# Norm sums as two matmuls with a tile of ones, rows placed later, and mLSTM preparation as a step of its own

## The chip, the cores and the metric

The kernel runs on one core of one Trainium2 chip. The metric is the device time of one execution in microseconds (us). Of the engines, PE multiplies matrices, DVE (VectorE) and ACT (ScalarE) do most elementwise work, POOL (GpSimd) a little of it, and SP only issues transfers. Each engine works off a queue of its own; the queues meet at semaphores.

## What is computed

One layer of an encoder block on 512 tokens of width 1024, in float32. Three mixers run side by side and are merged by gates.

```python
h = rms_norm(x, mix_norm_g[l])
proj = h @ w_in[l]
ml_q, ml_k, ml_v, ml_o, ml_gates, na_qkv, xa_q, merge_pre = jnp.split(proj, split_points, axis=-1)
y_ml = mlstm_branch(ml_q, ml_k, ml_v, ml_o, ml_gates, ...)
y_na = neighbourhood_attention(na_q, na_k, na_v, na_rpb[l])
mem_k, mem_v = jnp.split(rms_norm(mem, mem_norm_g[l]) @ w_mem_kv[l], 2, axis=-1)
y_xa = memory_cross_attention(xa_q, mem_k, mem_v)
merged = g_ml * (y_ml @ w_br_ml[l]) + g_na * (y_na @ w_br_na[l]) + g_xa * (y_xa @ w_br_xa[l])
x = x + merged @ w_out[l]
x = x + conv_glu_ffn(rms_norm(x, ffn_norm_g[l]), w_ffn_up[l], ...)
return rms_norm(x, final_norm_g)
```

Here `rms_norm` multiplies each token by the reciprocal root of its mean square plus 1e-6. The mLSTM branch has 4 heads of width 128 and runs in both directions; each head's 512 tokens are worked on in 4 chunks.

## The kernel before

Activations lie transposed, features on the partitions and tokens along the free axis. Every operand of a projection is split into a rounded part and the rest (`split_act` for activations: ACT copies, L209, DVE subtracts, L210; `emit_split` for weights: L185 on ACT, L186 on DVE), and each product is three matmuls (`mm3`, L203 to L205). A block of weights is loaded by SP (tile `wr`, three buffers) three blocks ahead, and split one block ahead into halves (tile `w`, four buffers). A projection `proj(key, ...)` is 8 steps over k, so 24 matmuls, of 512 columns for x and 256 for the memory tokens. The blocks come in this order: mlq (four columns of a k at a time, into four banks `mm`), mlk0 to mlk3, tm (values and gates), xaq0 to 3, o0 to o3 (output gate), memk0 to 3, memv, naq, nak, the merge gates with the branch products, out, then the FFN (ua, uu, dn).

The norm is not applied to the operand. Squares are summed over the 8 feature tiles into `acc` (tokens on the free axis), and the sum over partitions is made later: `rstd_cols` gets one column per 128 tokens (a float32 matmul with one column of ones, L285, which the profile shows as two records each), DVE scales and adds the epsilon (L287) and POOL raises to the power -0.5 (L289). `rstd_row` turns these columns into a row that stands on all partitions: two diagonal tiles (L302), two matmuls with a tile of ones (L303), a copy by ACT (L305). The row multiplies what a projection gives. That is done three times: for x inside mlk0, for the memory tokens between o1 and o3, for the FFN in its first block.

The mLSTM runs as a generator, `ml_all`. After each projection block the main program calls `step(RB)` or `step(RM)`, which adds 1.4 or 0.75 to a quota and lets the generator run to its next `yield` for each whole one. `ml_prep` makes the decays; its rows go out to DRAM (`rd`) and come back on all partitions as tiles R, loaded by SP (L564), to which POOL adds a mask (L567), giving a second tile of the same tag, four buffers in all, so one head's worth. Each head then does: `keys` (products of keys and queries, L586; keys transposed, L588, copied by ACT with a scale, L590, and by DVE, L591), `diagonal` (exponentials of the masked R by ACT, L600, times the products, L604), `states` (L626, three matmuls per direction, the first result copied by ACT, L629, the others added by DVE, L631), `queries` (exponentials of R, L613), and four times `values_J` (L642, L644) with a normalisation (L646 to L653). The next head's R is loaded right after `queries`. `emit_y` ends a head one head later: transposes (L668), a product with the gate (L670), and a split.

A scheduler orders the instructions of each engine by a model of its own; `tc.issue_after` puts instructions behind a named one.

Of the kernel before, what the change touches and what calls it, by code (L numbers as in the profile page):

```python
# [17 lines left out]
P = 128  # L18
S = 512
# [83 lines left out]
def hybrid_block(ctx, tc, xT, memT, wflat, vecs, gbias, nabias, outa, outb):  # L103
# [14 lines left out]
    def nm(s):  # L118
        uid[0] += 1
        return f"{s}_{uid[0]}"  # L120
# [13 lines left out]
    def atps():  # L134
        return atp.tile([P, 512], F32, tag="at", name=nm("at"))
# [141 lines left out]
    V.tensor_scalar(ngh, vec[:, VEC["mlng"]:VEC["mlng"] + 4], 0.5, None, op0=ALU.mult)  # L277


    def rstd_cols(acc, ntok, tag, n=D):  # L280

        nt = ntok // P
        ps = atps()
        for t in range(nt):
            PE.matmul(ps[:, t:t + 1], acc[:, t * P:(t + 1) * P], ones[:, 0:1], start=True, stop=True)  # L285
        v = tiny(nt)
        V.tensor_scalar(v, ps[:, :nt], 1.0 / n, EPS, op0=ALU.mult, op1=ALU.add)  # L287
        col = cp.tile([P, nt], F32, name=f"rc_{tag}")
        G.tensor_tensor(col, v, nhalf[:, :nt], op=ALU.pow)  # L289
        return col  # L290
# [54 lines left out]
    for k in range(KT):  # L345
# [6 lines left out]
        for f in range(4):  # L352
            fs = slice(f * P, (f + 1) * P)
            mm3(ps_q[f], wh[:, fs], wl[:, fs], XH[k], XL[k], k == 0, k == KT - 1)

    ps_k = [proj(("mlk", 0), XH, XL, bank=atps, at={1: lambda: norm.append(rstd_cols(acc, S, "x")),
                                                    7: lambda: norm.append(rstd_row(norm[0], S, "x"))})]
    rc, rb = norm
    ps_k.append(proj(("mlk", 1), XH, XL, bank=atps))
    rcc = cp.tile([P, NT], F32, name="rcc")  # L360
    V.tensor_scalar(rcc, rc, C_ML, None, op0=ALU.mult)

# [98 lines left out]
    ml = {}  # L461


    def ml_prep():
        gv = Gt.rearrange("p t (d k h) -> p t d k h", d=2, k=2)
        T4 = lambda a: a.rearrange("p (t d h) -> p t d h", t=4, d=2)
        f = tiny(32)
# [55 lines left out]
        V.tensor_tensor(rr[:36], cu[:36], mr[:36], op=ALU.subtract)  # L523
        for d in range(2):
            G.dma_start(rd[d], rr[32 * d:32 * d + 4, :])
        yield
        for d in range(2):
            for u in range(2):
                g = 2 * u + d
                gs = slice(32 * g, 32 * g + 4)  # L530
                ends = mr[gs].rearrange("p (t c) -> p t c", t=NT)[:, :, P - 1 if d == 0 else 0:][:, :, 0:1]
                V.tensor_tensor(dg[gs, g], ends.to_broadcast([4, NT, 4]),
                                ident[gs, gs].unsqueeze(1).to_broadcast([4, NT, 4]), op=ALU.mult)
# [17 lines left out]
            J, Jp = pr[d]  # L551
            V.tensor_tensor(ex[:, 1, d, J], en[:, 1, d, J], mb[:, d, Jp], op=ALU.add)
        A.activation(ex, ex, AF.Exp)
        ml.update(rd=rd, em=em, bi=bi, mb=mb, ex=ex)

    def ml_all():
        yield from ml_prep()
        rd, em, bi, mb = ml["rd"], ml["em"], ml["bi"], ml["mb"]

        def load_R(h):  # L560
            R, rm = [], []
            for d in range(2):
                t = tp.tile([P, S], F32, tag="R", name=nm("R"), bufs=4)
                SY.dma_start(t, rd[d, h].partition_broadcast(P))  # L564
                R.append(t)
                t = tp.tile([P, S], F32, tag="R", name=nm("R"), bufs=4)
                G.tensor_tensor(t.rearrange("p (j c) -> p j c", j=4), R[d].rearrange("p (j c) -> p j c", j=4),  # L567
                                msk[d].unsqueeze(1).to_broadcast([P, 4, P]), op=ALU.add)
                rm.append(t)
            return R, rm  # L570
# [93 lines left out]
        def emit_y(h, H):  # L664
# [8 lines left out]
                yml.extend([unit(F32R), unit(F32R)])  # L673
            split_act(yml[0][:, hs], yml[1][:, hs], y)

        prev = None
        R, rm = load_R(0)
        for h in range(4):
            kt, C = own(h)
            kq = keys(h, kt)  # L680
# [247 lines left out]
        mem_part(f)  # L928
        step(RB)
    for f in range(4):  # L930
        ps = proj(("o", f), XH, XL)
        t = scr()
        V.tensor_tensor(t, ps, rb, op=ALU.mult)
        A.activation(t, t, AF.Tanh, scale=0.5)
        if f == 0:
            so.append(unit())
        if f == 1:

            with tc.issue_after(st["mm"]):
                mrc = rstd_cols(macc, M, "m")  # L940
        if f == 2:
            mrb = rstd_row(mrc, M, "m")
        V.tensor_scalar(so[0][:, f * S:(f + 1) * S], t, 1.0, None, op0=ALU.add)
        step(RB)
    mkv = unit()
    mk, mv = mkv[:, 0:1024], mkv[:, 1024:2048]
    for f in range(4):
        ps = proj(("memk", f), MH, ML, M)
        V.tensor_tensor(mk[:, f * M:(f + 1) * M], ps[:, :M], mrb, op=ALU.mult)
        step(RM)  # L950
    pss = [mmps() for _ in range(2)]
    for i in range(4):
# [216 lines left out]
    for hh in range(2):  # L1169
# [3 lines left out]
        for j in range(HF):  # L1173
            f = HF * hh + j
            if f == 0:
                wa, wu = weights(("ua", f)), weights(("uu", f))
                pa, pu = mmps(), mmps()
                for k in range(KT):
                    if k < KT - 1:
                        mm3(pa, wa[k][0], wa[k][1], HH[k], HL[k], k == 0, False)  # L1180
                for k in range(KT - 1):
                    mm3(pu, wu[k][0], wu[k][1], HH[k], HL[k], k == 0, False)
                k = KT - 1
                mm3(pa, wa[k][0], wa[k][1], HH[k], HL[k], False, True)
                rc2 = rstd_cols(acc2, S, "2")
                mm3(pu, wu[k][0], wu[k][1], HH[k], HL[k], False, True)
            else:
                pa = pa1 if f == 1 else proj(("ua", f), HH, HL)
            if f == 0:
                pa1 = proj(("ua", 1), HH, HL)  # L1190
                rb2 = rstd_row(rc2, S, "2")
            c = conv(pa, rb2, "ffw", "ffb", f, FT)
            sq = scr()
            A.activation(sq, c, AF.Square)
# [131 lines left out]
```

## Time and profile before

| what | us |
|---|---|
| median of 3 runs | 887.96 |
| lowest and highest | 886.85, 888.22 |
| profiled execution | 888.33 |
| its span, first to last instruction | 886.5 |
| PE busy in the span | 875.3 |
| DVE, ACT, POOL busy | 580.3, 449.8, 165.6 |

Bytes moved to and from HBM are 98.9 MB, 112 GB/s over the span. In the profile, times in the lists of waits are the engine's idle time before a line, with what released it; a matmul's duration is that of its whole passage and longer than its distance to the next start, because matmuls overlap.

### The profile page before, as it was taken

The numbers are of one execution on the slowest core, as the hardware profiler recorded it, in microseconds if no ns is written. First come the engines' busy times: TensorE is split into PE (matmuls) and PEld (weight loads), VectorE is DVE, ScalarE is ACT, GpSimd is POOL, SyncE is SP. The second block draws the span as 40 slices with busy tenths as digits, with TensorE's granted clock in tenths as the row PEclk, the third lists the DMA queues.
The fourth block names the chain that finished last, engine by engine and source line by source line (L and its number), as shares of the span: only waits on it lengthen the run. The fifth ranks groups of instructions, "written<-read, shape, count | busy, mean of one in ns | idle before, by whom it ended". The sixth has DMA issues, their size and how long they took to land.

```text
span 886.5 us, 12192 instructions
## 1 busy us (share of the span) xinstructions
PE 875.3 (99%) x4342; PEld 741.6 (84%) x4342; DVE 580.3 (65%) x1153; ACT 449.8 (51%) x955; POOL 165.6 (19%) x238
## 2 busy tenths in 40 slices
PE   9999999999999999999999999999999999999997
PEld 7898877988888888888888888888888888888897
DVE  6794576766566747988767557667733466667433
ACT  7453446654345638888744435454422344444532
POOL 4201222110000930543000211211100011111010
PEclk9999999999999999999999999999999999999999
DMA  7324643532222534554333432232233322332412
GB/s 257 103 81 132 197 146 100 165 115 76 72 89 80 131 106 126 157 142 138 111 98 109 141 106 88 98 116 95 66 99 97 119 95 95 97 98 84 140 33 95
DMA packets 39436, 99.67 MB, mean 112 GB/s; under 512 B 5960, under 2 KB 13640, under 8 KB 39376
## 3 DMA queue, kind: packets, MB, share of 16 engines
q1 hardware_dynamic: 31728, 92.45, 32.0%
q0 software_dynamic: 7360, 6.32, 3.3%
q8 instruction: 34, 0.56, 0.3%
q14 instruction: 26, 0.21, 0.1%
q10 hardware_dynamic: 288, 0.14, 0.1%
HBM read 94.67 MB, written 4.21 MB: 112 GB/s over the span
## 4 chain that ended last, share of the span: by engine, by line
PE 94%; DMA 2%; DVE 1%; issue 1%; ACT 1%; POOL 0%; SPq 0%; POOLq 0%; DVEq 0%; ACTq 0%
PE mm L205 28%; PE mm L203 28%; PE mm L204 28%; PE at L203 2%; PE at L205 2%; PE at L204 2%; DMA R<-rd 1%; PE at L783 1%; PE at L764 1%; PE at L642 1%; PE at L644 1%; DMA s<-xT 1%; DMA rd<-s 0%; PE at L626 0%; PE at L745 0%
## 5 line engine op out<-in xcount | busy, mean ns | idle before, releaser
L203 PE MATMUL mm<-u,w 128*128 128x512 f32 (+1 forms) x1077 | 417.7, 388 | 0.4 <-ACT u L209 0.4
L205 PE MATMUL mm<-u,w 128*128 128x512 f32 (+1 forms) x1077 | 414.1, 384 | 0.1
L204 PE MATMUL mm<-u,w 128*128 128x512 f32 (+1 forms) x1077 | 413.7, 384 | 0.1
L185 ACT ACTIVATE w<-wr 128x512 fp32r<-128x512 f32 (+1 forms) x298 | 184.4, 623 | 239.7 <-PE mm L205 209.1
L186 DVE TENSOR_TENSOR w<-wr,w 128x512 fp32r<-128x512 f32 (+3 forms) x299 | 213.7, 716 | 114.4 <-ACT w L185 112.2
L205 PEld LDWEIGHTS mm<-u,w 128*128 128x128 f32 x1077 | 202.4, 188 | 40.8 <-DVE w L186 0.7
L203 PEld LDWEIGHTS mm<-u,w 128*128 128x128 f32 x1077 | 202.6, 188 | 39.6 <-ACT u L209 0.7
L204 PEld LDWEIGHTS mm<-u,w 128*128 128x128 f32 x1077 | 202.6, 188 | 39.2 <-DVE u L210 0.5
L1198 POOL TENSOR_TENSOR s<-s,rb 128x512 f32<-128x512 f32 x22 | 37.3, 1695 | 252.5 <-DVE s L1197 240.0
L457 POOL DMA_DIRECT2D u<-nav_d x128 | 62.2, 518 | 96.8 <-PE at L783 57.6
L209 ACT ACTIVATE u<-s 128x512 fp32r<-128x512 f32 x26 | 16.4, 631 | 55.3 <-DVE s L1201 54.5
L1201 DVE TENSOR_TENSOR s<-mm,s 128x512 f32<-128x512 f32 x22 | 15.2, 691 | 23.3 <-POOL s L1198 23.3
L1044 POOL TENSOR_TENSOR acc<-acc,s 128x512 f32<-128x512 f32 x7 | 9.1, 1295 | 102.7 <-ACT s L1043 102.7
L371 ACT ACTIVATE s<-pad,vec 128x512 f32<-128x512 f32 x30 | 24.4, 813 | 7.0 <-DVE pad L369 6.4
L210 DVE SCALAR_TENSOR_TENSOR u<-s,u 128x512 fp32r<-128x512 f32 x26 | 18.0, 691 | 14.7 <-ACT u L209 14.7
L372 DVE SCALAR_TENSOR_TENSOR s<-pad,vec,s 128x512 f32<-128x512 f32 x30 | 22.5, 751 | 4.3 <-ACT s L371 4.2
L1197 DVE SCALAR_TENSOR_TENSOR s<-s,s 128x512 f32<-128x512 f32 x22 | 15.2, 692 | 14.0 <-ACT s L1196 14.0
L373 DVE SCALAR_TENSOR_TENSOR s<-pad,vec,s 128x512 f32<-128x512 f32 x30 | 22.5, 751 | 0.9
L1196 ACT ACTIVATE s<-s 128x512 f32<-128x512 f32 x22 | 13.9, 632 | 16.3 <-DVE s L1195 16.2
L203 PE MATMUL mm<-w,u 128*128 128x512 f32 x48 | 19.0, 395 | 0.0
L205 PE MATMUL mm<-w,u 128*128 128x512 f32 x48 | 18.7, 390 | 0.0
L204 PE MATMUL mm<-w,u 128*128 128x512 f32 x48 | 18.7, 390 | 0.0
(285 smaller groups left out, 1028.1 us busy)
## 6 DMA issues: line engine op xcount, KB each, us to landing
wr<-wflat SPq DMA_DIRECT2D x140, 512.0 KB, 3.3
s<-xT SPq DMA_DIRECT2D x16, 256.0 KB, 4.4
nab<-nabias SPq DMA_DIRECT2D x16, 256.0 KB, 2.7
u<-nav_d POOLq DMA_DIRECT2D x128, 32.0 KB, 2.5
wr<-wflat SPq DMA_DIRECT2D x15, 192.0 KB, 2.4
nav_d<-nv POOLq DMA_DIRECT2D x8, 256.0 KB, 2.4
R<-rd SPq DMA_DIRECT2D x8, 256.0 KB, 3.8
wr<-wflat SPq DMA_DIRECT2D x2, 544.0 KB, 3.3
```

Of the source, the lines that this page charges most:

```text
L185: A.activation(h[:, u:v], src, AF.Copy)
L186: V.tensor_tensor(l[:, u:v], src, h[:, u:v].bitcast(F32), op=ALU.subtract)
L203: PE.matmul(ps, lh, rh, start=start, stop=False)
L204: PE.matmul(ps, lh, rl, start=False, stop=False)
L205: st["mm"] = PE.matmul(ps, ll, rh, start=False, stop=stop).ins
L209: A.activation(h, src, AF.Copy, scale=scale)
L210: V.scalar_tensor_tensor(l, src, scale, h.bitcast(F32), op0=ALU.mult, op1=ALU.subtract)
L371: A.activation(t1, pad[:, 0:512], AF.Identity, scale=vcol(w, i), bias=vcol(b, i))
L372: V.scalar_tensor_tensor(t1, pad[:, 1:513], vcol(w, n + i), t1, op0=ALU.mult, op1=ALU.add)
L373: V.scalar_tensor_tensor(t1, pad[:, 2:514], vcol(w, 2 * n + i), t1, op0=ALU.mult, op1=ALU.add)
L457: G.dma_start(vw[r * 32:(r + 1) * 32, i * 256:(i + 1) * 256], nav_v[hf, r, CW[b]:CW[b] + 32, hp * 256:(hp + 1) * 256])
L1198: G.tensor_tensor(c, c, rb2, op=ALU.mult)
```

## The change

`rstd_cols` is cut in two. `rstd_parts` splits the sums of squares into two rounded parts (one ACT copy, one DVE subtraction). `rstd_cols` multiplies both with a tile of ones (L291), so the sum over partitions stands on every partition for every token, and DVE takes each 128 columns times the identity and sums along the row, which picks the columns (L295); the scale and the epsilon go into the same instruction. POOL's power is L298 now.

The places change too. For x, the columns come after the fourth k of mlk0 (before: after the second), the row after the fourth k of mlk1 (before: at the end of mlk0). For the memory tokens the parts are made ahead of o2, the columns inside o2, the row in memk0, and the explicit order is gone. For the FFN the parts come before the last k of the first block, the columns after the first k of ua1, the row behind ua1 as before.

In the mLSTM, the load of head 0's R moves from after the preparation to the start of its last step, and that step now ends with a `yield`, so that head 0's keys and first diagonal come one step of the generator later, and so does everything behind them.

```diff
...
     V.tensor_scalar(ngh, vec[:, VEC["mlng"]:VEC["mlng"] + 4], 0.5, None, op0=ALU.mult)
-    def rstd_cols(acc, ntok, tag, n=D):
+    def rstd_parts(acc, ntok):
+
+        h, l = [sp.tile([P, 512], F32R, tag="scr", name=nm("s"))[:, :ntok] for _ in range(2)]
+        split_act(h, l, acc)
+        return h, l
+
+    def rstd_cols(parts, ntok, tag, n=D):
         nt = ntok // P
         ps = atps()
+        for i, part in enumerate(parts):
+            PE.matmul(ps[:, :ntok], onesr, part, start=i == 0, stop=i == 1)
+        v = tiny(nt)
+        d = scr(P)
         for t in range(nt):
-            PE.matmul(ps[:, t:t + 1], acc[:, t * P:(t + 1) * P], ones[:, 0:1], start=True, stop=True)
-        v = tiny(nt)
-        V.tensor_scalar(v, ps[:, :nt], 1.0 / n, EPS, op0=ALU.mult, op1=ALU.add)
+            V.tensor_tensor_reduce(d, ps[:, t * P:(t + 1) * P], ident, 1.0 / n, EPS, ALU.mult, ALU.add,
+                                   accum_out=v[:, t:t + 1])
         col = cp.tile([P, nt], F32, name=f"rc_{tag}")
         G.tensor_tensor(col, v, nhalf[:, :nt], op=ALU.pow)
         return col
...
             fs = slice(f * P, (f + 1) * P)
             mm3(ps_q[f], wh[:, fs], wl[:, fs], XH[k], XL[k], k == 0, k == KT - 1)
-    ps_k = [proj(("mlk", 0), XH, XL, bank=atps, at={1: lambda: norm.append(rstd_cols(acc, S, "x")),
-                                                    7: lambda: norm.append(rstd_row(norm[0], S, "x"))})]
+    xp = rstd_parts(acc, S)
+    ps_k = [proj(("mlk", 0), XH, XL, bank=atps, at={3: lambda: norm.append(rstd_cols(xp, S, "x"))}),
+            proj(("mlk", 1), XH, XL, bank=atps, at={3: lambda: norm.append(rstd_row(norm[0], S, "x"))})]
     rc, rb = norm
-    ps_k.append(proj(("mlk", 1), XH, XL, bank=atps))
     rcc = cp.tile([P, NT], F32, name="rcc")
     V.tensor_scalar(rcc, rc, C_ML, None, op0=ALU.mult)
...
     ml = {}
-    def ml_prep():
+    def ml_prep(load_R):
         gv = Gt.rearrange("p t (d k h) -> p t d k h", d=2, k=2)
         T4 = lambda a: a.rearrange("p (t d h) -> p t d h", t=4, d=2)
         f = tiny(32)
...
         V.tensor_tensor(rr[:36], cu[:36], mr[:36], op=ALU.subtract)
         for d in range(2):
             G.dma_start(rd[d], rr[32 * d:32 * d + 4, :])
+        ml["rd"] = rd
         yield
+        ml["R"] = load_R(0)
         for d in range(2):
             for u in range(2):
                 g = 2 * u + d
...
             J, Jp = pr[d]
             V.tensor_tensor(ex[:, 1, d, J], en[:, 1, d, J], mb[:, d, Jp], op=ALU.add)
         A.activation(ex, ex, AF.Exp)
-        ml.update(rd=rd, em=em, bi=bi, mb=mb, ex=ex)
+        ml.update(em=em, bi=bi, mb=mb, ex=ex)
+        yield
     def ml_all():
-        yield from ml_prep()
-        rd, em, bi, mb = ml["rd"], ml["em"], ml["bi"], ml["mb"]
         def load_R(h):
+            rd = ml["rd"]
             R, rm = [], []
             for d in range(2):
                 t = tp.tile([P, S], F32, tag="R", name=nm("R"), bufs=4)
...
                 yml.extend([unit(F32R), unit(F32R)])
             split_act(yml[0][:, hs], yml[1][:, hs], y)
+        yield from ml_prep(load_R)
+        em, bi, mb = ml["em"], ml["bi"], ml["mb"]
         prev = None
-        R, rm = load_R(0)
+        R, rm = ml["R"]
         for h in range(4):
             kt, C = own(h)
             kq = keys(h, kt)
...
         mem_part(f)
         step(RB)
     for f in range(4):
-        ps = proj(("o", f), XH, XL)
+        if f == 2:
+            mp = rstd_parts(macc, M)
+        ps = proj(("o", f), XH, XL, at={3: lambda: norm.append(rstd_cols(mp, M, "m"))} if f == 2 else {})
         t = scr()
         V.tensor_tensor(t, ps, rb, op=ALU.mult)
         A.activation(t, t, AF.Tanh, scale=0.5)
         if f == 0:
             so.append(unit())
-        if f == 1:
-
-            with tc.issue_after(st["mm"]):
-                mrc = rstd_cols(macc, M, "m")
-        if f == 2:
-            mrb = rstd_row(mrc, M, "m")
         V.tensor_scalar(so[0][:, f * S:(f + 1) * S], t, 1.0, None, op0=ALU.add)
         step(RB)
+    mrc = norm[2]
     mkv = unit()
     mk, mv = mkv[:, 0:1024], mkv[:, 1024:2048]
     for f in range(4):
-        ps = proj(("memk", f), MH, ML, M)
-        V.tensor_tensor(mk[:, f * M:(f + 1) * M], ps[:, :M], mrb, op=ALU.mult)
+        ps = proj(("memk", f), MH, ML, M, at={3: lambda: norm.append(rstd_row(mrc, M, "m"))} if f == 0 else {})
+        V.tensor_tensor(mk[:, f * M:(f + 1) * M], ps[:, :M], norm[3], op=ALU.mult)
         step(RM)
     pss = [mmps() for _ in range(2)]
     for i in range(4):
...
                         mm3(pa, wa[k][0], wa[k][1], HH[k], HL[k], k == 0, False)
                 for k in range(KT - 1):
                     mm3(pu, wu[k][0], wu[k][1], HH[k], HL[k], k == 0, False)
+                p2 = rstd_parts(acc2, S)
                 k = KT - 1
                 mm3(pa, wa[k][0], wa[k][1], HH[k], HL[k], False, True)
-                rc2 = rstd_cols(acc2, S, "2")
                 mm3(pu, wu[k][0], wu[k][1], HH[k], HL[k], False, True)
             else:
                 pa = pa1 if f == 1 else proj(("ua", f), HH, HL)
             if f == 0:
-                pa1 = proj(("ua", 1), HH, HL)
-                rb2 = rstd_row(rc2, S, "2")
+                pa1 = proj(("ua", 1), HH, HL, at={0: lambda: norm.append(rstd_cols(p2, S, "2"))})
+                rb2 = rstd_row(norm[4], S, "2")
             c = conv(pa, rb2, "ffw", "ffb", f, FT)
             sq = scr()
             A.activation(sq, c, AF.Square)
```

Lines of the new kernel that the text below names, with those of the old: L548/L550 were L537/L539, L578 (POOL's mask) was L567, L597/L599 (keys) were L586/L588, L601 (copy of transposed keys) was L590, L611 (diagonal) was L600, L624 (queries) was L613, L637 (states) was L626, L640 was L629, L653/L655 (values) were L642/L644, L657 to L664 (normalisation) were L646 to L653, L312 (row) was L303, L949 (tanh of o) was L934, L1005 (tanh of a gate) was L995.

On PE, around o0 and o1 (before: mm_1294 and mm_1363; after: mm_1276 and mm_1338), the order of before:

```order
L205 MATMUL mm_1194<-u_149,w_1138 128x512
L537 MATMUL at_1234<-ident,s_1120 128x100 x4
L539 MATMUL at_1239<-dg,ones 128x64
L586 MATMUL at_1263<-u_437,u_438 128x128 x4
L588 MATMUL at_1264<-ident,u_438 128x128 x4
L203 MATMUL mm_1294<-u_148,w_1188 128x512
...
L205 MATMUL mm_1294<-u_149,w_1191 128x512
L626 MATMUL at_1324<-u_573,u_1262 128x129 x3
L626 MATMUL at_1331<-u_573,u_1262 128x129 x3
L203 MATMUL mm_1363<-u_148,w_1288 128x512
```

and of after:

```order
L205 MATMUL mm_1200<-u_149,w_1144 128x512
L548 MATMUL at_1248<-ident,s_1126 128x100 x4
L550 MATMUL at_1253<-dg,ones 128x64
L203 MATMUL mm_1276<-u_148,w_1194 128x512
...
L597 MATMUL at_1307<-u_443,u_444 128x128 x4
L599 MATMUL at_1308<-ident,u_444 128x128 x4
L203 MATMUL mm_1338<-u_148,w_1270 128x512
...
L205 MATMUL mm_1338<-u_149,w_1273 128x512
L637 MATMUL at_1367<-u_579,u_1306 128x129 x3
L637 MATMUL at_1374<-u_579,u_1306 128x129 x3
L653 MATMUL at_1408<-u_579,E_1323 128x129 x2
```

Keys stand one block later, between o0 and o1, and states with the first values behind o1, ahead of o2 (mm_1432).

On ACT, the same place. E_1279 and E_1338 in before are head 0's diagonals, u_1262 its copies of keys, E_1345 and E_1350 its queries, E_1565 head 1's first diagonal. Before:

```order
L600 ACTIVATE E_1279<-R_1260,bi 128x128
L590 ACTIVATE u_1262<-at_1264,ex 128x128
L600 ACTIVATE E_1279<-R_1260,bi 128x128
L600 ACTIVATE E_1338<-R_1256,bi 128x128
L590 ACTIVATE u_1262<-at_1264,ex 128x128
L600 ACTIVATE E_1338<-R_1260,bi 128x128
L600 ACTIVATE E_1338<-R_1256,bi 128x128
L590 ACTIVATE u_1262<-at_1264,ex 128x128
L600 ACTIVATE E_1338<-R_1260,bi 128x128
L613 ACTIVATE E_1345<-R_1254,en 128x128 x3
L613 ACTIVATE E_1350<-R_1258,en 128x128 x3
L185 ACTIVATE w_1357<-wr_1186 128x512
```

After; E_1388 and E_1393 are head 0's queries, u_1306 its copies of keys and, from L640 on, its states, E_1646 and E_1709 the diagonals of head 1:

```order
L185 ACTIVATE w_1335<-wr_1192 128x512
L949 ACTIVATE s_1301<-s_1301 128x512
L611 ACTIVATE E_1646<-R_1400,bi 128x128 x2
L601 ACTIVATE u_1306<-at_1308,ex 128x128
L611 ACTIVATE E_1709<-R_1400,bi 128x128 x2
L601 ACTIVATE u_1306<-at_1308,ex 128x128
L611 ACTIVATE E_1646<-R_1404,bi 128x128 x2
L601 ACTIVATE u_1306<-at_1308,ex 128x128
L185 ACTIVATE w_1426<-wr_1268 128x512
L611 ACTIVATE E_1709<-R_1404,bi 128x128 x2
L185 ACTIVATE w_1429<-wr_1268 128x512
L640 ACTIVATE u_1306<-at_1367 128x129
```

The copies of the keys stood among head 0's own exponentials; now each of the three stands behind exponentials of head 1.

On PE, the norm of the memory tokens. Before, inside o3 (mm_1507), among the values of head 0:

```order
L205 MATMUL mm_1507<-u_148,w_1436 128x512
L303 MATMUL at_1474<-s_1475,onesr 128x256
L642 MATMUL at_1486<-u_573,E_1338 128x129
L303 MATMUL at_1474<-s_1479,onesr 128x256
L644 MATMUL at_1486<-u_1262,E_1345 128x129
L642 MATMUL at_1486<-u_573,E_1338 128x129
L644 MATMUL at_1486<-u_1262,E_1350 128x129
```

After, the sums inside o2 (mm_1432), the row at the seam of memk0 (mm_1554) and memk1 (mm_1603):

```order
L203 MATMUL mm_1432<-u_149,w_1335 128x512
L291 MATMUL at_1445<-s_1420,onesr 128x256
L204 MATMUL mm_1432<-u_151,w_1335 128x512
L291 MATMUL at_1445<-s_1421,onesr 128x256
L205 MATMUL mm_1432<-u_149,w_1335 128x512
...
L204 MATMUL mm_1554<-u_576,w_1488 128x256
L312 MATMUL at_1571<-s_1572,onesr 128x256
L205 MATMUL mm_1554<-u_575,w_1488 128x256
L203 MATMUL mm_1603<-u_575,w_1548 128x256
L312 MATMUL at_1571<-s_1576,onesr 128x256
L204 MATMUL mm_1603<-u_576,w_1548 128x256
```

The row's matmuls moved by more than one block.

## The prediction

> **What bounds the kernel now.** I read the page first: how busy each engine is, then its chain.
>
> ```profile
> span 886.5 us, 12192 instructions
> PE 875.3 (99%) x4342; PEld 741.6 (84%) x4342; DVE 580.3 (65%) x1153; ACT 449.8 (51%) x955; POOL 165.6 (19%) x238
> PE 94%; DMA 2%; DVE 1%; issue 1%; ACT 1%; POOL 0%; SPq 0%; POOLq 0%; DVEq 0%; ACTq 0%
> ```
>
> PE is busy 99% of the span and makes 94% of the chain. So the time moves only with PE's own work, or with what it waits for inside that work. The second view is the list of PE's waits.
>
> ```profile
> PE at L626 <- ACT u L590: 1.7, 3, 1.0
> PE at L303 <- DVE s L302: 1.2, 1, 1.2
> PE at L644 <- DVE u L631: 0.8, 1, 0.8
> ```
>
> These three are all that lies between PE's first matmul and its last worth speaking of: 3.7 us as listed. I then looked at the stretches of the timeline that hold them, since a wait also costs the restart of the pipeline. Columns: start, duration.
>
> ```profile
> 125.69 0.39 PE L204 MATMUL mm<-u,w 128*128 128x512 f32 x1
> 125.92 0.39 PE L205 MATMUL mm<-u,w 128*128 128x512 f32 x1
> 127.31 0.49 PE L626 MATMUL at<-u,u 128*128 128x129 f32 x2 [1.00 <-ACT u L590]
> 128.14 0.49 PE L626 MATMUL at<-u,u 128*128 128x129 f32 x2 [0.34 <-ACT u L590]
> 128.98 1.40 PE L626 MATMUL at<-u,u 128*128 128x129 f32 x8 [0.35 <-ACT u L590]
> 130.13 0.47 PE L203 MATMUL mm<-u,w 128*128 128x512 f32 x1
> ...
> 135.66 0.50 PE L285 MATMUL at<-ones,acc_m 128*128 128x1 f32 x4
> 136.02 0.69 PE L642 MATMUL at<-u,E 128*128 128x129 f32 x4
> 137.53 0.46 PE L644 MATMUL at<-u,E 128*128 128x129 f32 x2 [0.81 <-DVE u L631]
> ...
> 145.33 0.39 PE L205 MATMUL mm<-u,w 128*128 128x512 f32 x1
> 146.96 0.39 PE L303 MATMUL at<-s,onesr 128*128 128x256 f32 x1 [1.25 <-DVE s L302]
> ```
>
> Matmuls of 512 columns start every 0.23 us (125.69 to 125.92). From L205 at 125.92 the states (L626) could have begun at 126.15 and begin at 127.31: 1.16 lost. Their 12 records take 2.82 us to 130.13. The last eight, with one wait ahead of them, take 1.15 to the next start, so twelve need 1.7 at most; at the 0.11 of an L642 record it would be 1.3. I take 1.5, so 1.3 more is lost, and call the states' stall 2.5. At L644, four L642 records end near 136.46 and L644 starts at 137.53: 1.07. At L303, 146.96 less 145.56 is 1.40. Together 5.0 us is the most that removing stalls can bring. All else the change can give is PE work.
>
> **The norm sums, PE's part.** Before, the sums are matmuls with one column, after, two with 512 (256 for mem).
>
> ```profile
> 29.42 0.95 PE L285 MATMUL at<-ones,acc_x 128*128 128x1 f32 x8
> 30.23 0.49 PE L203 MATMUL at<-u,w 128*128 128x512 f32 x1
> 30.55 0.40 PE L204 MATMUL at<-u,w 128*128 128x512 f32 x1
> ...
> 526.09 0.94 PE L285 MATMUL at<-ones,acc 128*128 128x1 f32 x8
> 526.90 0.49 PE L203 MATMUL mm<-u,w 128*128 128x512 f32 x1
> ```
>
> Eight records cost 0.81 us to the next start, and that one is followed after 0.32, not 0.23: 0.90. Two matmuls at 0.23 cost 0.46. So -0.45 for x and -0.45 for the ffn norm. For mem, four records (135.66 to 136.02, 0.36) become two of 256 columns, about 0.12 each: -0.12.
>
> The Trainium skill bears on this price (TensorE: Matmul & The Clock Gate, Back-to-back issue gap): it puts a sustained stream of 512-column matmuls with weight loads at about 131 ns each. By it the four new 512-column matmuls would cost 0.52 and not 0.91, and the sum would be 0.4 lower. The rows say 0.23, so the measurement decides.
>
> **The norm sums, the other engines.** Each split is one ACT copy and one DVE subtraction (for mem 256 columns); then DVE picks the diagonal, four times for x and ffn, twice for mem. The trace has no such reduce on 128 columns. Its nearest rows are the same instruction on 256 columns, with its read of the accumulator, and the diagonals' products on 128 without a reduction:
>
> ```profile
> L750 DVE CUSTOM_DVE_ANT_0 s<-at,nab x32: 414/419/426, 330.5 to 432.6; 128x256 f32<-128x256 f32 x32
> L750 DVE DVE_READ_ACCUMULATOR2_ANT y<- x32: 81/84/86, 330.9 to 432.9; 128x1 f32 x32
> 32.03 1.66 DVE L302 TENSOR_SCALAR s<-ident,y 128x128 fp32r<-128x128 f32 x8
> 30.65 1.03 POOL L289 TENSOR_TENSOR rc_x<-y,nhalf 128x4 f32<-128x4 f32 x1 [4.40 <-DVE y L287]
> ```
>
> Between 0.21 (1.66/8) and 0.50 (419+84 ns) each; I take 0.35, since half the columns of L750 are read, and all four write one scratch tile. Four make 1.4 us (0.8 to 2.0), where one tensor_scalar of 0.16 stood. From the last sum to the last diagonal that is about 0.4 (PE's end) +1.4+0.25+1.03+0.2+0.3+1.66 = 5.2 us. For x, sums come after the fourth k of mlk0 and the row after the fourth of mlk1: 24 matmuls between, 5.4 us. It fits barely, and two weight splits of 0.69 may stand among it on DVE: 0.25 taken for a wait (0 to 1.4). The row comes 12 matmuls, 2.7 us, later, and so do the convolutions that free mlq's banks:
>
> ```profile
> 35.92 0.69 DVE L369 TENSOR_TENSOR pad<-mm,rb_x 128x512 f32<-128x512 f32 x1
> ```
>
> The first bank would be free at 35.92+0.69+2.7 = 39.3, and mlk2, which takes it, begins at about 40 (30.23, 18 more matmuls of mlk0, the pair, 24 of mlk1), so mlk1 covers it, with some 0.7 to spare; if that cover goes, each us late is a us on PE. x: -0.45+0.25 = -0.2. The ffn norm has the same distance (after k=0 of ua1 to its end, 21 matmuls, 4.8 us) and its split stands ahead of the last k of ua0: -0.45+0.25 = -0.2.
>
> **Mem norm.** Its row moves from inside o3, three matmuls in, to the seam of memk0 and memk1, so the 1.40 at L303 goes. In its place come three smaller risks. The sums (L291) now stand ten matmuls behind L655, inside o2, but the copy of the sum of squares stands on ACT behind head 0's first normalisation (L657, L661, L664), a chain in which each step waits for DVE: +0.4 (0 to 1.5). The row's L312 comes between memk0 and memk1, with 23 matmuls of 256 columns before it (2.8 us), and its products stand on DVE behind head 0's next normalisations: +0.35 (0 to 1.0). Then ACT's copy of the row stands ahead of a weight split of memk2 and behind exponentials of head 2 that wait for POOL: +0.4 (0 to 1.5). Sum -1.40-0.12+1.15 = -0.4.
>
> **Preparation in a step of its own.** Keys of head 0 (L597, L599) move from ahead of o0 to behind it, states from ahead of o1 to behind it. Nothing is added on PE. Each queue it passes: SP's loads and POOL's rows stand in the same sequence as before, but ACT's don't. The copies of the transposed keys (L590, now L601), for which states wait, stood among head 0's exponentials (L600, now L611). Now all three stand behind the first exponentials of head 1. What those cost is seen in before:
>
> ```profile
> 126.60 0.40 ACT L600 ACTIVATE E<-R,bi 128x128 f32<-128x128 f32 x1 [1.10 <-POOL R L567]
> 126.91 0.35 ACT L590 ACTIVATE u<-at,ex 128x128 f32<-128x128 f32 x1
> ...
> 128.57 0.35 ACT L590 ACTIVATE u<-at,ex 128x128 f32<-128x128 f32 x1
> 128.82 0.39 ACT L600 ACTIVATE E<-R,bi 128x128 f32<-128x128 f32 x1
> 129.12 1.86 ACT L613 ACTIVATE E<-R,en 128x128 f32<-128x128 f32 x6
> 130.87 0.62 ACT L185 ACTIVATE w<-wr 128x512 fp32r<-128x512 f32 x1
> 133.94 0.69 ACT L600 ACTIVATE E<-R,bi 128x128 f32<-128x128 f32 x2 [2.44 <-POOL R L567]
> ...
> 135.06 0.26 ACT L629 ACTIVATE u<-at 128x129 f32<-128x129 f32 x1
> ```
>
> ```profile
> 129.15 1.30 SPq L564 DMA_DIRECT2D R<-rd  x2
> 132.61 2.56 POOL L567 TENSOR_TENSOR R<-R,msk 128x512 f32<-128x512 f32 x2 [6.05 <-DMA R<-rd]
> ```
>
> Head 1's masked row can't be earlier than its R: that load starts at 129.15, when head 0's exponentials (last L600, 128.82) free a buffer, lands 3.4 us later, and POOL needs 1.3 for each of two. So ACT stands until 133.94, though the L590s are not hurt, being ahead. In after, head 0's exponentials still start at 126.60 (POOL sets that, not PE), and the last of them stays within 0.5 us of 128.82: so ACT still stands to about 133.9. The first L601 follows two exponentials, 134.3; the second, 135.2; the third stands behind the second masked row (132.61+2.56 = 135.17) and two more exponentials: 136.0. PE reaches states 5.5 us later than in before, by the 24 matmuls of o1 (130.13 to 135.66): 126.15+5.5 = 131.6. The three states of the second direction need the third copy's partner on DVE (0.35 behind it, 136.7) and take 0.6, so states end at 137.3 where 133.1 was possible: a stall of 4.2 against 2.5, +1.7.
>
> Their copies (L640) then stand behind two weight splits and two exponentials on ACT, as L629 (135.06) stood behind L600 in before, and DVE's additions behind them, so L655 starts near 140.0, while PE gets there, over two L653 and six matmuls, at 138.8: 1.2 against 1.07, +0.1.
>
> The tail of the branch shifts by one step too: the last head's output (emit_y) now stands behind the tanh of gate 1.
>
> ```profile
> 250.59 0.63 ACT L209 ACTIVATE u<-s 128x512 fp32r<-128x512 f32 x1 [0.53 <-DVE s L670]
> 251.19 0.72 ACT L995 ACTIVATE s<-s,mgbh 128x512 f32<-128x512 f32 x1
> ```
>
> ```profile
> 251.69 0.62 PE L203 MATMUL mm<-u,w 128*128 128x512 f32 x2
> ```
>
> PE uses that copy at 251.69 without a wait. Behind the tanh of 0.72 it comes up to 0.7 later, part of which the earlier gate product saves: +0.2 (0 to 0.7).
>
> **Sum.** x -0.2, ffn -0.2, mem -0.4, states +1.7, L655 +0.1, tail +0.2: +1.2. The profiled execution took 888.33 us, 1.83 around its span and 0.37 above the median of the three runs (887.96). 888.33+1.2 = 889.5; I say 889.8, since the waits of mem and x, taken near their lower ends, have more room above than below.
>
> **Rivals.** What a run of this kernel can tell from no change is about 0.2%, 1.8 us: the bounds are 886.2 and 889.7.
>
> (a) Head 1's rows come before PE needs states. This ends faster. The place is the first L611 of head 1 on ACT, and the price is all of the 3.6 us stalled at L626 and L644 in before, and the 1.8 I add. If POOL's second row is done by 131, no stall is left: 888.33-0.2-0.2-0.4+0.2-3.6 = 884.1, the 1.8 not arising. For it: a buffer's last reader in after may come a microsecond before 128.82, and each microsecond there is one less for PE. Against it: 1.3+1.3 on POOL and 3.4 for the load, 6 us, start no earlier than 126.6. At some 1.7 us earlier the states' stall equals that of before, and the gain is that of the norms. Chance of ending faster this way, in whole or by half: 0.27.
>
> (b) The stalls at states come out as in before, or the mem norm's new waits cancel its gain less than I think: 886.5 to 889.5. The change then does not do on the chip what the order alone shows, the wait having only changed place. Chance 0.26.
>
> (c) The late ACT queue is not made up: after states, ACT has the splits of o3 and memk behind it, and the mem norm's chain stands in the same queue. Each of the three mem waits at its upper end (1.5+1.0+1.5 instead of 1.15) gives +2.9, so 892.5. For it: L629 and L934 in before were late in the same way. Against: PE has 24 matmuls of 0.23 in each o block to cover them. Chance 0.12.
>
> My forecast, around 889.8 to 891, has 0.35. So faster 0.27, same 0.26, slower 0.47. The range leaves out the best of (a) and the worst of (c): 885.0 to 892.8.
>
> **What would show it.** In the profile of after: PE's wait at L637 for ACT L601 should sum to 3.5 us or more, in place of 1.7; ACT should idle before the first L611 of head 1 until 133 to 134; L655 should wait for DVE; the wait at L312 should be under 1.0, and the 1.25 at L303 be gone; L291's pairs should take 0.46. A wait at L637 under 1.5 would make it (a). A new wait at an ordinary L203 for a weight split in memk would make it (c).

## The result

The changed kernel takes 889.27 us (median of 20 runs, 887.70 to 892.41) against 887.79 (median of 20, 886.81 to 888.83): a ratio of 1.0017, 95% interval 1.0010 to 1.0024. It is slower by 1.5 us, clear of noise, and that lies just inside the 0.2% that the prediction called no change; 889.8 was forecast, with slower by over 0.2% the likeliest.

The profile of one run of it (889.31 us), read as before: the page, then the list of PE's waits.

```profile
span 887.5 us, 12182 instructions
PE 877.4 (99%) x4328; PEld 743.3 (84%) x4328; DVE 585.0 (66%) x1173; ACT 450.6 (51%) x958; POOL 163.7 (18%) x238
...
PE at L637 <- ACT u L601: 1.7, 3, 1.0
PE at L312 <- DVE s L311: 1.0, 1, 1.0
```

The three waits became two. The one at the states has its old size, 1.7 in three pieces. The one at the row of the memory norm went from 1.2 to 1.0, in a new place. L655 (L644 of old) waits no more. The timeline of PE at the states shows what took that wait's place. Columns: start, duration.

```profile
132.38 0.39 PE L205 MATMUL mm<-u,w 128*128 128x512 f32 x1
133.74 0.49 PE L637 MATMUL at<-u,u 128*128 128x129 f32 x2 [0.98 <-ACT u L601]
134.58 0.49 PE L637 MATMUL at<-u,u 128*128 128x129 f32 x2 [0.35 <-ACT u L601]
135.45 1.77 PE L637 MATMUL at<-u,u 128*128 128x129 f32 x8 [0.38 <-ACT u L601]
137.01 1.07 PE L653 MATMUL at<-u,E 128*128 128x129 f32 x4
137.73 0.78 PE L203 MATMUL mm<-u,w 128*128 128x512 f32 x1
138.30 0.63 PE L204 MATMUL mm<-u,w 128*128 128x512 f32 x1
138.73 0.63 PE L205 MATMUL mm<-u,w 128*128 128x512 f32 x1
...
140.22 0.49 PE L655 MATMUL at<-u,E 128*128 128x129 f32 x2
```

From 137.73 on, 512-column matmuls start 0.43 to 0.57 us apart, not 0.23. Cut into stretches of 1 us (width, PE busy, granted clock, DMA share, GB/s), the reason stands in the clock's column:

```profile
135.00:136.00 1.00, 0.62 (x4) 1.00 0.32 123
136.00:137.00 1.00, 1.00 (x6) 0.58 0.40 137
137.00:138.00 1.00, 1.00 (x7) 0.50 0.01 2
138.00:139.00 1.00, 1.00 (x4) 0.50 0.28 41
139.00:140.00 1.00, 1.00 (x4) 0.71 0.76 258
140.00:141.00 1.00, 1.00 (x5) 1.00 0.56 225
```

The clock is halved for 3.4 us (136.16 to 139.57). The fall begins inside the thin stretch in which PE waits and runs only small matmuls (132.6 to 137.7; in before such a stretch lies from 126.15 to 130.13, and the clock stays at 1.00). One such window takes 0.002 from a run's mean granted clock. The mean of a single run tells little, since the clock also falls behind PE's last matmul, in the tail; on average over the runs it was 0.9974 for the changed kernel and 0.9984 for before. The queue on ACT stands as the order showed it:

```profile
128.46 1.85 ACT L624 ACTIVATE E<-R,en 128x128 f32<-128x128 f32 x6
130.22 0.62 ACT L185 ACTIVATE w<-wr 128x512 fp32r<-128x512 f32 x1
130.74 0.61 ACT L949 ACTIVATE s<-s 128x512 f32<-128x512 f32 x1
132.74 0.69 ACT L611 ACTIVATE E<-R,bi 128x128 f32<-128x128 f32 x2 [1.39 <-POOL R L578]
133.34 0.35 ACT L601 ACTIVATE u<-at,ex 128x128 f32<-128x128 f32 x1
...
135.03 0.37 ACT L601 ACTIVATE u<-at,ex 128x128 f32<-128x128 f32 x1
...
137.81 0.26 ACT L640 ACTIVATE u<-at 128x129 f32<-128x129 f32 x1
```

ACT idles for head 1's masked row until 132.74, and the copies for which PE waits stand behind. On DVE, the chain to L655 ends at 140.16 (L642), whatever PE does until then:

```profile
137.76 0.34 DVE L642 SCALAR_TENSOR_TENSOR u<-u,ex,at 128x129 f32<-128x129 f32 x1
138.02 1.25 DVE L952 TENSOR_SCALAR u<-s 128x512 f32<-128x512 f32 x1
139.18 0.98 DVE L642 SCALAR_TENSOR_TENSOR u<-u,ex,at 128x129 f32<-128x129 f32 x3
```

So what the slow clock takes here is time in which L655 would have waited.

### The profile page after: what moved, and what is told of

It is laid out like the page before. It is cut to its first block, busy times and chain, and to the rows that moved or that the text cites. A ratio compares the mean times of both kernels' runs of the same rounds, so it can differ in the third digit from the quotient of the medians.

```text
span 887.5 us, 12182 instructions
## 1 busy us (share of the span) xinstructions
PE 877.4 (99%) x4328; PEld 743.3 (84%) x4328; DVE 585.0 (66%) x1173; ACT 450.6 (51%) x958; POOL 163.7 (18%) x238
## 4 chain that ended last, share of the span: by engine, by line
PE 95%; DMA 2%; DVE 1%; issue 1%; ACT 1%; POOL 0%; POOLq 0%; SPq 0%; ACTq 0%; DVEq 0%
PE mm L203 28%; PE mm L204 28%; PE mm L205 28%; PE at L203 2%; PE at L205 2%; PE at L204 2%; DMA R<-rd 1%; PE at L796 1%; PE at L777 1%; PE at L653 1%; PE at L637 1%; PE at L655 1%; PE at L758 0%; PE at L759 0%; PE at L884 0%
## 5 line engine op out<-in xcount | busy, mean ns | idle before, releaser
L578 POOL TENSOR_TENSOR R<-R,msk 128x512 f32<-128x512 f32 x8 | 11.6, 1451 | 41.6 <-ACT E L624 24.9
L203 PE MATMUL mm<-w,u 128*128 128x512 f32 x48 | 19.0, 395 | 0.0
L205 PE MATMUL mm<-w,u 128*128 128x512 f32 x48 | 18.7, 390 | 0.0
```

The source lines that it names most:

```text
L203: PE.matmul(ps, lh, rh, start=start, stop=False)
L205: st["mm"] = PE.matmul(ps, ll, rh, start=False, stop=stop).ins
```

## The experiments

The theory: the order on ACT (copies of head 0 behind exponentials of head 1) costs time at states, the new place of the memory norm costs a wait, and PE's own work in the norms falls by about 1 us. Rivals: the norms' new form costs more than it saves; the fallen clock is the cost; states wait for something else.

### Each part alone

The first kernel is the kernel before with only the mLSTM hunks of the diff, the second the changed kernel with those hunks taken back.

> The old norms, the mLSTM part of the change alone. If the late copies of the keys and the fallen clock are what costs, this carries the loss: 0.8 to 2 us slower than before (888.6 to 889.8 against 887.8), the states' waits 2.0 to 2.6 in three pieces, a granted clock below 1.000 in most runs. If the norm part carries the loss, this is within 0.5 us of before.

> The new norms, the mLSTM preparation as before. By the terms of PE's work (x and ffn -0.45 each, mem -0.12, the wait at L303 of 1.25 against one of 0.99 at L312) this is 0.8 to 1.3 us faster than before (about 886.8), with the granted clock as in before. If the sums through the tile of ones cost more than they save, it is not faster.

The mLSTM part alone: 888.68 us, ratio 1.0005 (0.9996 to 1.0014). The norms alone: 887.73, ratio 0.9996 (0.9986 to 1.0005). Neither is told from before, and both differences are smaller than expected: 0.6 above and 0.35 below the runs of before beside them (888.08), where 0.8 to 2 and 0.8 to 1.3 were named. Added they make 1.0001, and the whole change 1.0017. The intervals leave room for some of that, but PE's waits, first of the mLSTM part, then of the norms, show that the parts don't add:

```profile
PE at L628 <- ACT u L592: 1.9, 3, 1.1
...
PE at L646 <- DVE u L633: 0.2, 1, 0.2
```

```profile
PE at L291 <- ACT s L209: 2.5, 1, 2.5
...
PE at L653 <- DVE u L640: 0.7, 1, 0.7
PE at L635 <- ACT u L599: 0.7, 2, 0.3
```

With the mLSTM part alone the old norm of the memory tokens has no wait at L303: its sums stand ahead of the states there, and states, values and o2 all lie between sums and row. So the step pays for its wait at the states (1.9) with the wait that it takes from L303. With the norms alone the split of the sum of squares comes late on ACT, behind the normalisation of head 0, and PE waits 2.5 at L291. This trace is the slowest of its 12 runs (889.52), so how much of the 2.5 a usual run has is not shown. In the changed kernel this wait is gone, and L312, which has none here, waits 1.0 there (the section on the old norm below shows for what). The saving at L303 could be had once, not twice.

### Keys ahead on ACT

```diff
+                ml["key", h] = A.activation(kt[:, 0, i], ...).ins
...
+                with tc.issue_after(ml["key", h - 1]) if h else ExitStack():
                     A.activation(E[:, i, :], rm[d][:, J * P:(J + 1) * P], AF.Exp, ...)
```

> The changed kernel, with the first diagonals of a head put on ACT behind the copies of the previous head's keys, by a NoSync edge and no other change. If the order on ACT is the cause, no wait stands at the states (before: 1.7 in three), the clock stays at 1.000, and the time falls by 2.5 to 4 us from the changed kernel, to 885.3 to 886.8, faster than both. If the states wait for something else as well (PE's products, DVE's partner copies), the time falls by less than 1 us.

889.60 us, ratio 1.0014 (1.0006 to 1.0023): no faster. Of the two expectations the second came true, that the states wait for something else as well, and the waits say for what:

```profile
PE at L657 <- DVE u L644: 2.2, 1, 2.2
PE at L639 <- ACT u L601: 1.4, 2, 0.9
```

The first copy came early, but each next one waited for DVE's partner copy into the same tile, and the copies of the states stood behind head 1's exponentials still: the wait moved to L657, which is L655 of the changed kernel. In its trace the clock stayed at 1.00 over this stretch, and the time is the changed kernel's.

### Keys and states ahead

```diff
             for i in range(3):
                 A.activation(kt[:, 0, i], pt[:, i * P:(i + 1) * P], AF.Copy, ...)
+            for i in range(3):
                 V.tensor_scalar(kt[:, 1, i], pt[:, (i + 1) * P:(i + 2) * P], ...)
...
+                        ml["st", h] = A.activation(C[:, d, i, 0:129], pv[:, i, 0:129], AF.Copy).ins
...
+                with tc.issue_after(ml["st", h - 1]) if h else ExitStack():
                     A.activation(E[:, i, :], rm[d][:, J * P:(J + 1) * P], AF.Exp, ...)
```

> The changed kernel; the exponentials of a head's first diagonal stand on ACT behind the copies of the previous head's keys and of its states, and the three ACT copies of the keys ahead of DVE's three. If the queue on ACT is the cause and the run with the keys alone ahead only moved the wait to L655 (its line there L657: 2.22), then neither wait is left (each under 0.6) and the time is 2 to 3.5 us under the changed kernel's, 886 to 887.3. If each wait only moves on to the next link of the same chain (DVE's partners, the normalisation), the gain stays under 1 us.

887.77 us, ratio 1.0000 (0.9990 to 1.0010), 1.5 under the changed kernel: less than the 2 to 3.5 expected if the queue on ACT were all, more than the 1 expected if each wait only moved on.

```profile
PE at L657 <- DVE u L644: 1.3, 1, 1.3
...
PE at L639 <- DVE u L603: 1.0, 1, 1.0
PE at L312 <- DVE s L311: 1.0, 1, 1.0
```

ACT no longer stands in any of these lines, though the waits add up to 3.3 us, where they were 2.7. What fell is not on the list. PE's clock stays at 1.00, and from the end of o1 to L657 (L655 of the changed kernel) PE takes 5.9 us in place of 7.6. A full clock alone brought nothing (the run above, and the one with filling matmuls below), so the gain is that DVE's chain to L657 ends earlier. Of this, 0.8 is one instruction on DVE: L954, which is L952 of the changed kernel, takes 0.41 in place of 1.25, because POOL's next addition now comes behind it, at 140.83. So the order on ACT, with what hangs on it, was worth 1.5 us. What is left is DVE, whose copies stand behind work of its own.

### The old norm for the memory tokens

```diff
-        if f == 2:
-            mp = rstd_parts(macc, M)
-        ps = proj(("o", f), XH, XL, at={3: lambda: norm.append(rstd_cols(mp, M, "m"))} if f == 2 else {})
+        ps = proj(("o", f), XH, XL)
...
+        if f == 1:
+            with tc.issue_after(st["mm"]):
+                mrc = rstd_cols1(macc, M, "m")
+        if f == 2:
+            mrb = rstd_row(mrc, M, "m")
...
-        ps = proj(("memk", f), MH, ML, M, at={3: lambda: norm.append(rstd_row(mrc, M, "m"))} if f == 0 else {})
+        ps = proj(("memk", f), MH, ML, M)
```

`rstd_cols1` is the function of before.

> The changed kernel, with the norm of the memory tokens as before: columns of ones behind o1, the row inside o3. In the run with the mLSTM part alone its matmuls stood without a wait. If the new place of the row costs its wait, L312's 0.99 goes and the time is 0.6 to 1.3 us under the changed kernel's, 888.0 to 888.7. If the wait comes back at the old place (1.25 in before), nothing is gained.

887.33 us, ratio 0.9998 (0.9989 to 1.0006): 1.9 under the changed kernel by the medians, 0.0019 or 1.7 us by the ratios, more than the wait alone and more than expected (0.6 to 1.3). Its only wait in this stretch is that at the states:

```profile
PE at L649 <- ACT u L613: 1.5, 3, 0.8
```

The new place and form of this one norm thus make up more than the whole loss. The traces say more on which of the two it is. From PE's 31st matmul of a projection to the last, this trace is 1.6 us shorter than that of the changed kernel, and 1.46 of it lie at the new place of the row: the first 28 matmuls of memk0 and memk1 take PE 4.89 us in the changed kernel and 3.43 here. Of the 1.46, 0.99 is the wait at L312, and most of the rest is the row's own two matmuls, which stand in o3 in this run. The row is made by the same function in both, so the wait comes with the place.

What makes the row late there is POOL. In the changed kernel its addition for a row of head 2 falls on DVE's diagonals (L311). The first row below is this addition. The second is the diagonals in the run with the norms alone, where the addition starts 8 us ahead of them, at 149.65:

```profile
154.97 1.65 POOL L578 TENSOR_TENSOR R<-R,msk 128x512 f32<-128x512 f32 x1 [9.53 <-ACT E L624]
...
157.50 0.87 DVE L311 TENSOR_SCALAR s<-ident,y 128x128 fp32r<-128x128 f32 x4
```

In the changed kernel the four diagonals take 1.90 in place of 0.87: the first of them takes 1.31 and ends at 156.71, just behind POOL, the others 0.28 each as usual. All five traces that have both the new memory norm and the mLSTM step show 1.9 at L311 and 0.99 at L312; the run with the norms alone has no wait at L312. So this wait comes neither from the norm's move alone nor from the step alone, and that is a second reason why the parts don't add.

### Both edits, and the other two norms

> Both edits at once: x and ffn norms new, mem norm as before, mLSTM step as in the changed kernel, keys and states ahead on ACT. If waits add, 884.8 to 886.5, faster than both kernels by 0.2% or more. If they share one cover, no better than the better of the two.

> The kernel with both edits, but the norms of x and of the FFN as before too: of the change only the mLSTM step is left, with keys and states ahead on ACT. By PE's work the new x and FFN norms are worth 0.8 to 0.9 us, so this is that much slower than the run with both edits beside it (0.05 to 0.15%), and still faster than before. If the sums through the tile of ones gain nothing, the two are the same.

> The kernel with both edits once more, beside the one above on the same chip: 0.15 to 0.3% faster than before, as it was.

Both edits together take 885.85 us (ratio 0.9977, 0.9965 to 0.9988) and, taken again, 886.07 (0.9978, 0.9970 to 0.9987): faster than both kernels, so the two savings add. Its waits when taken again, and then those of the kernel with the old norms throughout (886.11, ratio 0.9986, 0.9977 to 0.9995):

```profile
PE at L651 <- DVE u L615: 1.4, 1, 1.4
...
PE at L669 <- DVE u L656: 1.2, 1, 1.2
```

```profile
PE at L648 <- DVE u L635: 1.2, 1, 1.2
PE at L630 <- DVE u L594: 1.1, 1, 1.1
```

The waits are alike; the ratios differ by 0.0008, which is 0.7 us for the new norms of x and of the FFN (forecast for PE's work 0.9, and 0.4 after waits), though the intervals of the two overlap. The traces settle it: PE goes from its 96th to its 145th matmul of a projection, with the norm of x between, in 12.23 or 12.24 us in all nine traces with the new norm and in 12.51 in all four with the old, and from its 2051st to its 2401st, with the norm of the FFN, in 80.24 to 80.29 against 80.74. So these two sums through the tile of ones save 0.28 and some 0.47 us, together 0.75 of the 0.9 that PE's rows said. The mLSTM step with the edges on ACT, under the old norms, is 0.14% faster than before. The edges without the step were not run, so what the step itself is worth stays open.

### PE filled while it waits

```diff
+            if h == 0:
+                fill = mmps()
+                with tc.issue_after(st["mm"]):
+                    for _ in range(5):
+                        last = PE.matmul(fill, onesr, XH[0], start=True, stop=True).ins
...
+                    with tc.issue_after(last) if h == 0 else ExitStack():
                         PE.matmul(pv[:, i, 0:129], kt[:, d, i], va[:, i + d, h, 0:129], start=True, stop=True)
```

> The changed kernel, with five more matmuls of 512 columns (of a tile of ones and a tile of x; the result is not used) between o1 and the states of head 0, where PE waits 0.98 us. They cost 1.14 us of PE time, of which the wait hides about 1. If the fall of the clock comes from a stretch in which PE does little, the clock falls in fewer runs or not at all. If the fall costs time beside the waits, the time is 0.5 to 1.5 us lower than the changed kernel's; if the wait for the copies of the states (L655) takes what the clock leaves, the time is the same within 0.5 us, though the clock is 1.000.

890.17 us, ratio 1.0024 (1.0013 to 1.0034). In its trace the clock stays at 1.00 over the stretch (granted clock behind the busy time, as above), and the wait comes back at L661, which is L655 of the changed kernel:

```profile
PE at L661 <- DVE u L648: 2.5, 1, 2.5
...
130.00:141.00 11.00, 7.89 (x41) 1.00 0.39 126
```

So a full clock bought nothing: the mean over its 12 runs was 0.9986, and by the ratios it is 0.6 us slower than the changed kernel, where the same within 0.5, or 0.5 to 1.5 less, was expected (the intervals of the two overlap). That agrees with the run with the keys ahead, which had the full clock and the same time. The fallen clock is a sign of the thin stretch and not the cost. That it costs nothing at all is not shown: the scheduler also put L661 behind four matmuls of o2, where L655 stands behind six.

### Second traces

> The kernel before, unchanged, for a second trace. In the five traces so far PE's 31st matmul of a projection starts at 12.7 to 13.1 or at 14.3 to 14.6 us, depending on when the clock comes to full speed. If that alone makes the runs of a kernel differ, the time from there to the last such matmul is 866.8 again, within 0.2. If waits inside differ from run to run (where the R loads land), it is not, and the waits at L626, L644 and L303 differ from 1.7, 0.8 and 1.2.

> The changed kernel for a second trace. L312's wait of 0.99 should be there again within 0.2, since all that it waits for hangs on PE and DVE; the waits at L637 may move by a microsecond with the time at which head 1's R lands, as they did in the second trace of before; the granted clock should be under 1.000 again, as in 20 of 20 runs.

The changed kernel (888.86 us) shows 1.6 at L637 and 1.0 at L312, and the same fall of the clock, as the first time. (L312 hangs on POOL too and not only on PE and DVE, but POOL's addition falls on the diagonals again, at 154.47.) (That a run's mean clock lies under 1.000, as the expectation wanted, is no sign of that fall: the second trace of before has 0.998, all of it in the tail.) The kernel before (887.77) doesn't:

```profile
PE at L303 <- DVE s L302: 1.2, 1, 1.2
...
PE at L626 <- ACT u L590: 0.7, 2, 0.3
PE at L644 <- DVE u L631: 0.5, 1, 0.5
```

2.4 us in place of the 3.7 from which the prediction started. From PE's 31st matmul of a projection to the last it takes 865.3 us, not 866.8, so the start alone doesn't make the runs differ. Two rows of the timeline, of PE and of ACT:

```profile
127.17 0.42 PE L626 MATMUL at<-u,u 128*128 128x129 f32 x2
...
126.39 0.40 ACT L600 ACTIVATE E<-R,bi 128x128 f32<-128x128 f32 x1 [1.20 <-POOL R L567]
```

In this run PE could begin the states at 127.17, 1.0 later than in the first (the full clock came later at the start), but ACT's exponentials came 0.2 earlier (126.60 in the first), so the wait before the first state was gone. What arrives from DRAM through POOL did not move with PE: here the start that was 1.0 later was more than given back (1.6 in the stretch above), and the first trace, with its early start, shows more wait than the second.

## Why the prediction was right, point by point

**Time.** 889.8 forecast, +1.2 by the sum; 889.27 measured, +1.5. The range held it, and slower was the right side, but the bound of 0.2% was just not reached, so the class given 0.47 did not come true by a hair and the one given 0.26 did. That one is rival (b), 886.5 to 889.5, and its text fits too: the wait at the states is 1.7 as in before, and the memory norm's new wait cancels its gain. The forecast starts from the profiled run, 0.37 over the median, and adds 0.3 for room; from the median the sum alone gives 889.2. That it lies so near the result is in part luck: the terms below are off both ways, the norms of x and of the FFN too dear, the memory norm too cheap.

**The norm's PE work.** Right. The reduce on 128 columns, taken at 0.35 between 0.21 and 0.50, is 0.29 with 0.08 for its read, 0.33 from one to the next:

```profile
L295 DVE CUSTOM_DVE_ANT_0 s<-at,ident x10: 283/291/292, 32.7 to 530.7; 128x128 f32<-128x128 f32 x10
L295 DVE DVE_READ_ACCUMULATOR2_ANT y<- x10: 82/82/83, 32.9 to 531.0; 128x1 f32 x10
```

The pairs of L291 for x and the FFN take the 0.46 that was named (0.45). Of the waits of 0.25 that were added for each, the FFN has none and x has 0.2: the row's two matmuls (L312) take 0.65 to the next start at 37.91, where L303 took 0.46 in before. These terms were -0.2 each and came out at -0.28 and -0.47, by the stretches above.

**Mem norm.** Here the sum was wrong in several places that partly cancelled. The wait at L312 was put at 0.35, for products behind head 0's normalisations, and is 0.99: DVE's first diagonal, held up beside POOL, ends at 156.7, where PE stands since 155.9. POOL is not in the prediction's term.

```profile
155.40 1.90 DVE L311 TENSOR_SCALAR s<-ident,y 128x128 fp32r<-128x128 f32 x4
157.05 0.36 PE L312 MATMUL at<-s,onesr 128*128 128x256 f32 x1 [0.99 <-DVE s L311]
```

The waits at L291 and for the splits of memk2, 0.4 each, are not in the list. The two sums themselves lengthen o2 by 0.57 (142.63 to 143.88, with three matmuls of 0.23 between), not 0.24, against 0.36 for the old ones: 0.2 dearer in place of 0.12 cheaper. And the 1.40 at L303 was credited to the norm's move, while the step alone takes it away too. So "-0.4 for the mem norm" fails as a step: against the same kernel with the old norm, the new one costs 1.7 to 1.9.

**States.** The order on ACT was read rightly, and the chip shows it: ACT idle before the first L611 of head 1, L601 behind it. The stall was put at 4.2. By the same measure, from the end of the large matmuls to the end of the states less 1.5 for their work, it is 2.9 (132.6 to 137.0), the first of the slow matmuls included; in waits it is 1.7. Head 1's row came at 132.74 and not 133.9, since its R load was issued 1.3 earlier (127.84; 129.15 in before), when a buffer came free: half of rival (a). And the base of 2.5, from which +1.7 was reckoned, is 1.3 in the second trace of before (127.17 to 129.93). So the term is +0.4 by the first trace and +1.6 by the second: both ends were too high, and the difference came out near only by the second. An estimate from the runs: the mLSTM part alone, with its gain of 1.40 at L303, is +0.6, so the rest of the step costs some 2, give or take the 0.8 of that ratio's interval.

**L655.** Forecast near 140.0, measured 140.22, by the chain that was named. The slow clock took up what would have been its wait, so the wait for DVE that was named as a sign is not in the list.

**Tail.** The 0.2 is not seen: no wait at the branch products stands in the list.

**What was not foreseen** is the clock, that POOL's addition would fall on the diagonals, and that the two parts of the change share one saving. The signs by which the prediction wanted to be judged: ACT idle until 133 (132.74, right); the 1.25 at L303 gone (right); L312 under 1.0 (0.99, just); L637 at 3.5 or more (1.7, wrong).

## What to carry to other kernels

An order by a scheduler is a place to look for head-of-line waits: ask for each instruction that PE waits for what stands ahead of it on its engine, and what that waits for. To put one link of such a chain ahead moves the wait to the next link; here an edge at the keys alone brought nothing, edges at keys and states 1.5 us, and with the old memory norm 3.3. Ask also what POOL will newly run beside a DVE instruction that PE waits for: such a meeting cost 1 us at the new place of the row. And a wait in one trace is a sample: take a second trace of the kernel before, ahead of any sum that starts from its waits.

## What the runs showed of the hardware

The TensorE clock fell to half for 3.4 us although PE never idled for longer than 1.1 us. It did so in both traces of the changed kernel and in the two experiments in which ACT kept this queue and nothing filled the wait; in all other traces the clock stayed at 1.00 there. Ahead of it lay 2.9 to 4.1 us of short waits and only small matmuls (of 129 columns, or of one). That length alone doesn't decide, since such stretches of up to 4.0 us (before) passed without a fall; what does is not shown. Averaged over their runs, the three kernels with this fall in the trace have 0.997, all others 0.998 to 0.999. The Trainium skill (TensorE: Matmul & The Clock Gate, What's actually happening) speaks of an idle window of about 3.4 us; the fall is as long as that in all four traces, but no idle time of that length stood ahead of it.

Two DVE instructions that multiply or add by a scalar and read no result of PE were held up where they fell together with POOL's addition. L952 took 1.25 at 138.02, beside this row of POOL, and 0.43 at 153.24; the first L311 took 1.31 at 155.40, and the ones behind it 0.28.

```profile
137.56 1.41 POOL L578 TENSOR_TENSOR R<-R,msk 128x512 f32<-128x512 f32 x1 [3.43 <-DMA R<-rd]
...
153.24 0.43 DVE L952 TENSOR_SCALAR u<-s 128x512 f32<-128x512 f32 x1
```

The Trainium skill (SBUF — State Buffer, Who interferes with whom) says that the two engines share a pair of ports that one of them holds for a whole instruction, and the rows agree: L952 ends 0.3 behind POOL's, the first L311 0.1 behind. Not every DVE instruction is held up: L642, which reads a result of PE, took 0.34 at 137.76 beside the same addition. L952 stood ahead of the last L642, so this is in the chain to L655, and L311 stood ahead of L312.
